# Value weights in column halves, a memory normalisation on ScalarE, and new ends for a two-layer decoder kernel

## The chip, the cores and the metric

The kernel runs on one core of a Trainium2 chip. The metric is the device time of one execution in microseconds. Before the change three runs gave a median of 1455.31 us, from 1453.81 to 1457.11 us.

## The reference, cut to what matters

The program is a decoder trunk of two layers on 256 tokens of width 1024, all in float32. Each layer is a half-step SwiGLU feed-forward part (FFN1), a mixer of four gated branches, a cross-attention into 256 memory tokens, and a second feed-forward part (FFN2). Each ends in `x = LayerNorm(alpha*x + f(x))`.

```python
mem_n = layer_norm(mem, mem_ln_g, mem_ln_b)            # once, for both layers
# mixer, branch a: local attention, 8 query heads on 2 key/value heads of 64, window 128, blocks of 128
p = exp(s - m); p = p / (sum(p) + exp(sink - m))
y_a = einsum('bngrqk,bnkgd->bnqgrd', p, vb).reshape(B, L, 512) @ swa_proj
# branch b: S5, a complex diagonal recurrence; branch d: differential attention
# branch c: gated depthwise convolution with 31 taps, LayerNorm over 512 channels, silu
y_c = conformer_conv(cu, ...) @ conv_proj
merged = g0 * y_a + g1 * y_b + g2 * y_c + g3 * y_d
x = layer_norm(alpha * x + merged @ w_out)
```

## The kernel before

**Weights.** Every large product is made of three TensorE passes (`mm3`): operands are split into a rounded part (hi) and the rest (lo), and hi*hi, hi*lo and lo*hi are added in PSUM. Weights come from HBM in raw halves of 128x1024, six at a time. For each half, called a split here and counted from 0 (236 per layer), ScalarE writes hi (a CAST) and VectorE writes lo (a TENSOR_TENSOR of the raw half and hi). `W.cap` bounds how many splits may be ahead of their use.

**Order.** All instructions are put in order when the program is built. A model of the engines' times (`Pace`, in `est`) is kept while instructions are issued; between matmuls `step()` looks whether the next task of a lane (local attention `swa`, differential attention `diff`, `s5`, `conv`, `taps`, the preparation lanes `prep`, `mem`, `bias`) is due by that model, and issues it. A task that says `yield` waits for its next turn. `ensure(name)` issues the rest of a lane at once. Taps of the convolution are put on VectorE (`fill`) when its modelled time falls behind TensorE's; what is left of them is flushed before the third gate's product, `gate(2)`. Each engine then runs its list strictly in that order, so a late instruction holds up all behind it.

**Local attention.** `swa_pv` multiplies the transposed probabilities (as the stationary operand, 128x128) with 64 columns of values (moving): 12 float32 matmuls per call, two calls per layer (query halves t = 0 and 1). ScalarE scales each 128x64 result by 1/sum into `osb`; `swa_end` transposes `osb` in eight blocks per layer and splits the result for `swa_proj`.

**Memory normalisation.** `mem_norm` runs once, in layer 0's FFN1, two row blocks: statistics and affine part on VectorE with gain and bias broadcast to two 512 KB tiles, then transposes, a split, and a store to DRAM that both cross-attentions read.

**Convolution.** After the flush, lane `conv` is issued within `gate(2)`, whose 96 matmuls are numbered from 0 here: `conv_norm` transposes the sum `c3` back to tokens (8 transposes), VectorE takes the statistics, GpSimd a power (`rstd`), ScalarE applies them (`Identity`, two of 512); `conv_act` transposes the result again (8 transposes); ScalarE makes a tanh and an affine copy (4 and 4 of 256, parameters `ph`), VectorE multiplies them, and both split them into `hT`, which `conv_proj`, the next product, reads.

**Ends.** The first product is `gate0` for token block c = 0: per chunk x-hi*w-hi and x-hi*w-lo, then all x-lo*w-hi at the end. The kernel's last work is the LayerNorm of token block 1 and four output stores from SyncE's queue.

Of the kernel before, what the change touches and what calls it, by code (L numbers as in the profile page):

```python
# [9 lines left out]
F32R = mybir.dt.float32r  # L10
# [3 lines left out]
ALU = mybir.AluOpType  # L14
# [168 lines left out]
def hybrid_decoder_kernel(ctx: ExitStack, tc: tile.TileContext, io, depth=DEPTH):  # L183
# [22 lines left out]
    def t2(dt=F32):  # L206
        return p2.tile([P, 512], dt, tag="s2", name="s2")
# [126 lines left out]

    def xs(xT, s, kc, c=None):

        if len(xT) == 3:
# [13 lines left out]
    class Norm:  # L351
# [22 lines left out]
        def finish(self, pump):  # L374
            self.scale()
            if pump:
                W.pump()
            self.apply(0)
            self.apply(1)
# [52 lines left out]
            run_task(name, q)  # L432


    def prod_tok(keys, xT, nk, before_c1=None, done=None, lo_last=False):

        hv = {}
        lo_last = lo_last or before_c1 is not None
        banks = [[None, None] for _ in keys]
        for c in range(2):  # L440
            for i, key in enumerate(keys):
                b = ps()
                for kc in range(nk):
                    if before_c1 and c == 0 and i == len(keys) - 1 and kc in (nk - 6, nk - 4):
                        before_c1((0,) if kc == nk - 6 else (1,))
                    if c == 0 and kc % 2 == 0:
                        hv[i, kc // 2] = W.take(key)
                    w = hv[i, kc // 2]
                    if lo_last and i == 0:
                        mm(b, xs(xT, 0, kc, c), w.h[:, kc % 2], kc == 0, False)  # L450
                        mm(b, xs(xT, 0, kc, c), w.l[:, kc % 2], False, False)
                        if kc == nk - 1:
                            for k in range(nk):
                                mm(b, xs(xT, 1, k, c), hv[i, k // 2].h[:, k % 2], False, k == nk - 1)
# [12 lines left out]
                if done:  # L467
                    done(i, c, b)
        return banks
# [18 lines left out]


    def ffn(xT, x, ln, before_c1, after_start=None, res=None, cap_end=CAP_FFN):  # L490
        gb, ub = prod_tok(("gate0", "up0"), xT, 8, before_c1)
        th = []
        for c in range(2):
            t = t2()
# [82 lines left out]
        for c in range(2):  # L577
            nm = block_norm(x[c], *w_ln)
            if c == 0:
                for h in range(2):  # L580
                    for (w2, gT), f in ((x_, f) for x_ in list(zip(ws, pend))[:-1] for f in range(2)):
                        out_mm(w2[f], gT, f, c, h)
                    if h == 0:
                        tick()
            for h in range(2):
                for i, (w2, gT) in enumerate(zip(ws, pend)):
                    if c == 0 and i < len(ws) - 1:
                        continue
# [9 lines left out]
            nm.finish(c == 1)  # L598
            if c == 0 and res is None:
                res = new_T()  # L600
        W.cap = CAP_FFN
# [4 lines left out]
    memD = dram.tile([P, 4096], F32, name="memT")  # L606

    def mem_norm():
        W.cap -= 2
        g, b = load_ln(io["mem_ln_g"], io["mem_ln_b"])  # L610
        mem = [t4(), t4()]
        for c in range(2):
            nc.sync.dma_start(out=mem[c], in_=m_in[0, c])
        yield 10.0
        for c in range(2):
            mt = mem[c]
            nm = Norm(mt, g, b, EPS)
            nm.half(0)
            nm.half(1)
            nm.scale()  # L620
            yield 1
            for h in range(2):
                nm.apply(h)
                yield 0
            for h in range(2):
                bk = transpose_blocks(mt[:, h * 512:(h + 1) * 512], 4)
                yield 0
                hi, lo = t2(F32R), t2(F32R)
                split_psum(bk, hi, lo)
# [4 lines left out]
        W.cap += 2  # L634

    memT = []

# [139 lines left out]
    def load_params():  # L777
# [4 lines left out]
        nc.sync.dma_start(out=rows[0:32], in_=io["s5_a_re"].rearrange("l (j a) p -> (l j) (a p)", a=2))  # L782
        nc.sync.dma_start(out=rows[32:64], in_=io["s5_a_im"].rearrange("l (j a) p -> (l j) (a p)", a=2))
        nc.sync.dma_start(out=rows[64:66], in_=io["diff_norm_g"])
        ls = sm(2)
        nc.sync.dma_start(out=ls[96:128], in_=io["s5_log_step"].rearrange("l (j a) -> (l j) a", a=2))
        r = 0
# [309 lines left out]
    def mixer(l, xT, x, before_c1, s5):  # L1097
# [324 lines left out]
        osb, dosb = [], []  # L1422

        def swa_scores(t, c):
            head = lambda r: (r // 2) * 4 + 2 * t + r % 2
# [9 lines left out]
        def swa_trans(t):  # L1435
            e0, e1, sums, d = att["a", t]
            r, o = inverse(sums, d), (t2(), t4())
            yield from transposed(o, e0, e1, 4)
            att["a", t] = (*o, r)

        def halves(o):
            if not o:
# [2 lines left out]
            return o  # L1445

        def swa_pv(t):
            halves(osb)
            o0, o1, r = att.pop(("a", t))
# [4 lines left out]
            for i in range(4):  # L1454
                g = i // 2
                for kb_ in range(2):
                    mm(b[:, 256 + i * 64:256 + (i + 1) * 64], o1[:, (2 * i + kb_) * P:(2 * i + kb_ + 1) * P], av[:, kb_, g * 64:(g + 1) * 64], kb_ == 0, kb_ == 1)
            yield 0
            for c in range(2):
                for k in range(4):  # L1460
                    S.activation(out=osb[c].rearrange("p (g u i d) -> p g u i d", g=2, u=2, i=2)[:, k // 2, t, k % 2],
                                 in_=b[:, c * 256 + k * 64:c * 256 + (k + 1) * 64], func=AF.Copy, scale=r[:, c * 4 + k:c * 4 + k + 1])

        def swa_end():
            aoT = L["aoT"] = (t4(F32R), t4(F32R))
            for c in range(2):
                b = transpose_blocks(osb[c], 4)
                yield 0
                o3 = [o.rearrange("p (k t) -> p k t", t=SEQ)[:, :, c * P:(c + 1) * P] for o in aoT]
                split_psum(b.rearrange("p (k t) -> p k t", t=P), o3[0], o3[1])  # L1470

        def attention_lane(name, scores, soft, mix, trans, pv, end):
            o = [(scores, 0, 1), (scores, 0, 0), (soft, 0), (scores, 1, 1), (scores, 1, 0), (mix, 0), (trans, 0), (soft, 1), (pv, 0), (mix, 1), (trans, 1), (pv, 1)]
# [3 lines left out]
            lane(name, [(("s", t) if f is scores else t, lambda f=f, t=t, k=k: f(t, *k)) for f, t, *k in o] + [(1, end)])  # L1477

        attention_lane("swa", swa_scores, swa_soft, None, swa_trans, swa_pv, swa_end)

        dkb = prod_feat("dk", xT, 8)
        dkT, dqT = t4(), t4()
# [86 lines left out]
        def project(key, oT, br, first=False):  # L1569
            gs = gates.pop(br)  # L1570
            if first:
                merged.extend([t4(), t4()])
            oT2 = [[oT[0]], [oT[1]], 1]
# [170 lines left out]
```

## Time and profile before

| | us |
|---|---|
| median of 3 runs (range) | 1455.31 (1453.81 to 1457.11) |
| the profiled execution | 1454.41 |
| its span in the trace | 1452.6 |
| TensorE busy | 1437.6 (99%) |
| VectorE busy | 1154.3 (79%) |
| ScalarE busy | 809.0 (56%) |
| GpSimd busy | 90.0 (6%) |
| HBM traffic | 188 GB/s over the span |

The span is the time from the first to the last instruction in the trace; 1.8 us of the execution lie around it. Busy time of TensorE counts pipelined matmuls and says that it is never idle for long, not that each matmul is as short as it can be. A row of a timeline gives start, length, engine, operation, output and inputs, and how many alike were joined; in brackets the idle time of that engine before the row and what ended it.

### The profile page before, as it was taken

What the parts mean: (1) busy time and instruction counts of PE and PEld (TensorE: products, weight loads), DVE (VectorE), ACT (ScalarE), POOL (GpSimd) and SP (SyncE); (2) the same over time, 40 slices, a digit from 0 to 9 for tenths busy, and PEclk for the clock granted to TensorE, in tenths of its full rate; (3) what the DMA queues carried; (4) which work ended last, traced back from release to release, by engine and by line L of the source; (5) the groups of instructions that cost most, each with busy time, mean ns of one, the idle gap of its engine ahead of it and who ended that gap; (6) DMA issues with size and microseconds to landing.
All of it is one profiled execution on the core that took longest, in us unless ns stands there. A gap on an engine that the chain in (4) does not pass through costs nothing.

```text
span 1452.6 us, 22933 instructions
## 1 busy us (share of the span) xinstructions
PE 1437.6 (99%) x8732; PEld 1236.0 (85%) x8732; DVE 1154.3 (79%) x1838; ACT 809.0 (56%) x1400; POOL 90.0 (6%) x113
## 2 busy tenths in 40 slices
PE   9999999999999999999999999999999999999997
PEld 6888889988887888888888888899888888888886
DVE  7789889898997878666788986839979887876665
ACT  6455543868956445444454555435988545444441
POOL 0300000101020000000000000010100300000000
PEclk9999999999999999999999999999999999999999
DMA  9766846544656756556665656555536577375650
GB/s 367 229 206 190 264 142 172 175 127 115 207 166 215 249 202 206 190 185 189 215 197 174 198 179 191 170 163 175 160 118 190 185 270 257 97 252 179 190 163 29
DMA packets 194197, 274.05 MB, mean 189 GB/s; under 512 B 38430, under 2 KB 118880, under 8 KB 194088
## 3 DMA queue, kind: packets, MB, share of 16 engines
q1 hardware_dynamic: 192488, 268.40, 58.1%
q0 software_dynamic: 1600, 4.20, 1.1%
q8 instruction: 68, 1.11, 0.3%
q14 instruction: 41, 0.34, 0.1%
HBM read 267.31 MB, written 5.24 MB: 188 GB/s over the span
## 4 chain that ended last, share of the span: by engine, by line
PE 92%; DVE 4%; ACT 2%; issue 1%; DMA 0%; SPq 0%; POOL 0%; POOLq 0%; DVEq 0%; ACTq 0%
PE b L177 92%; DVE s L177 4%; ACT s L177 2%; DMA raw<-in_ffn_w_in_dram 0%; DVE sm L177 0%; POOL sm L177 0%; SPq L69 0%; POOLq L1740 0%; DVE gpad L177 0%; DVEq L177 0%; SPq L285 0%; SPq L283 0%; ACTq L177 0%
## 5 line engine op out<-in xcount | busy, mean ns | idle before, releaser
L177 PE MATMUL b<-s,s 128*128 128x512 f32 (+3 forms) x8272 | 1405.6, 336 | 3.3 <-ACT s L177 1.8
L177 PEld LDWEIGHTS b<-s,s 128*128 128x128 f32 (+1 forms) x8272 | 1184.5, 183 | 192.2 <-issue 5.8
L177 DVE TENSOR_TENSOR s<-raw,s 128x1024 fp32r<-128x1024 f32 x472 | 570.3, 1232 | 114.5 <-ACT s L177 111.3
L177 ACT CAST s<-raw 128x1024 fp32r<-128x1024 f32 x472 | 483.1, 1055 | 62.8 <-DMA raw<-in_mix_w_in_dram 22.9
L177 ACT COPY s<-b 128x256 f32<-128x256 f32 (+2 forms) x216 | 93.9, 441 | 257.8 <-PE b L177 249.4
L177 DVE TENSOR_TENSOR s<-b,s 128x256 f32<-128x256 f32 (+3 forms) x264 | 115.2, 459 | 99.4 <-ACT s L177 91.5
L177 DVE TENSOR_TENSOR s<-s,s 128x512 f32<-128x512 f32 (+8 forms) x206 | 150.3, 735 | 35.4 <-ACT s L177 30.9
L177 ACT CAST s<-b 128x256 fp32r<-128x256 f32 (+1 forms) x100 | 36.9, 421 | 113.1 <-PE b L177 113.0
L177 POOL TENSOR_TENSOR sm<-sm,mhalf 128x1 f32<-128x1 f32 (+2 forms) x24 | 28.3, 1179 | 922.1 <-DVE sm L177 921.9
L177 ACT CAST s<-s 128x512 fp32r<-128x512 f32 x44 | 29.0, 669 | 93.2 <-DVE s L177 82.3
L177 ACT ACTIVATE s<-gpad,pc 128x256 f32<-128x256 f32 x152 | 66.2, 524 | 16.6 <-DVE gpad L177 16.6
L177 PE MATMUL b<-ident,s 128*128 128x128 f32 x449 | 64.9, 273 | 2.0 <-ACT s L177 1.9
L177 PEld LDWEIGHTS b<-ident,s 128*128 128x128 f32 x449 | 54.0, 141 | 12.6 <-ACT s L177 2.5
L177 DVE SCALAR_TENSOR_TENSOR s<-s,sm,s 128x512 f32<-128x512 f32 x72 | 52.5, 748 | 6.3 <-POOL sm L177 4.9
L177 ACT ACTIVATE s<-b,sm 128x64 f32<-128x64 f32 (+3 forms) x68 | 21.8, 396 | 47.9 <-DVE sm L177 43.8
L177 DVE SCALAR_TENSOR_TENSOR s<-gpad,pc,s 128x256 f32<-128x256 f32 x96 | 47.0, 541 | 0.6
L177 ACT ACTIVATE s<-b 128x512 f32<-128x512 f32 (+1 forms) x68 | 33.2, 533 | 13.1 <-PE b L177 13.1
L177 DVE SCALAR_TENSOR_TENSOR s<-s,s 128x512 f32<-128x512 f32 (+1 forms) x56 | 37.7, 685 | 0.4 <-ACT s L177 0.3
L177 ACT ACTIVATE s<-s 128x512 f32<-128x512 f32 (+1 forms) x52 | 32.2, 639 | 1.7 <-DVE s L177 1.7
L177 DVE SCALAR_TENSOR_TENSOR s<-s,b 128x512 f32<-128x512 f32 x40 | 26.2, 678 | 5.4 <-PE b L177 5.4
L177 ACT ACTIVATE s<-s,sm 128x128 f32<-128x128 f32 x64 | 28.4, 453 | 1.4 <-DVE sm L177 1.4
L177 DVE SCALAR_TENSOR_TENSOR s<-b,s 128x512 f32<-128x512 f32 x32 | 22.0, 687 | 8.2 <-PE b L177 8.1
(92 smaller groups left out, 305.5 us busy)
## 6 DMA issues: line engine op xcount, KB each, us to landing
raw<-in_ffn_w_in_dram SPq DMA_DIRECT2D x176, 512.0 KB, 3.9
raw<-in_mix_w_in_dram SPq DMA_DIRECT2D x116, 512.0 KB, 4.3
raw<-in_ffn_w_out_dram SPq DMA_DIRECT2D x88, 512.0 KB, 3.4
raw<-in_mix_w_out_dram SPq DMA_DIRECT2D x16, 512.0 KB, 5.2
raw<-in_cross_wkv_dram SPq DMA_DIRECT2D x16, 512.0 KB, 5.0
raw<-in_mix_w_in_dram SPq DMA_DIRECT2D x32, 128.0 KB, 4.3
raw<-in_swa_proj_dram SPq DMA_DIRECT2D x8, 512.0 KB, 5.2
raw<-in_diff_proj_dram SPq DMA_DIRECT2D x8, 512.0 KB, 5.1
```

Of the source, the lines that this page charges most:

```text
L177: return f(*a, **k)
```

## The change

1. `swa_trans` scales the probabilities by 1/sum before their transposes: four 128-wide ACTIVATEs on ScalarE and one 1024-wide multiply on VectorE per call. `swa_pv` makes the 64 value columns the stationary operand, placed at array columns 0 or 64 (`at=(0, 64*i)`), and the probabilities the moving one. The result is already transposed; it is split from PSUM, and `swa_end` with its transposes is gone.
2. `mem_norm` takes mean and variance with two ScalarE passes and normalises there; gain and bias come as columns of `pa` and are applied by ScalarE after the transposes. The two broadcast loads are gone, two loads of eight rows into `rows` are added, and `W.cap` is lowered by 1 instead of 2 meanwhile.
3. `gate0`, c = 0: first x-hi*w-hi and x-lo*w-hi for all chunks, then all x-hi*w-lo.
4. The last LayerNorm issues both subtract-and-scale steps before both steps with the power's result; the last output quarter is stored from ScalarE's queue.

```diff
@@ def swa_trans(t):
+            for i in range(4):
+                S.activation(out=e0[:, i * P:(i + 1) * P], in_=e0[:, i * P:(i + 1) * P], func=AF.Copy, scale=r[:, i:i + 1])
+            tt(V, e1.rearrange("p (i k) -> p i k", i=4), e1.rearrange("p (i k) -> p i k", i=4), r[:, 4:8].unsqueeze(2).to_broadcast([P, 4, 256]), ALU.mult)
+            yield 0
             yield from transposed(o, e0, e1, 4)
@@ def swa_pv(t):
-            for i in range(4):
-                g = i // 2
-                mm(b[:, i * 64:(i + 1) * 64], o0[:, i * P:(i + 1) * P], av[:, 0, g * 64:(g + 1) * 64])
...
+            for g in range(2):
+                for i in range(2):
+                    r = 2 * g + i
+                    mm(b[64 * i:64 * i + 64, g * 256:g * 256 + P], av[:, 0, g * 64:(g + 1) * 64], o0[:, r * P:(r + 1) * P], g == 0, True, skip=True, at=(0, 64 * i))
                 for kb_ in range(2):
-                    mm(b[:, 256 + i * 64:256 + (i + 1) * 64], o1[:, (2 * i + kb_) * P:(2 * i + kb_ + 1) * P], av[:, kb_, g * 64:(g + 1) * 64], kb_ == 0, kb_ == 1)
-            yield 0
-            for c in range(2):
-                for k in range(4):
-                    S.activation(out=osb[c].rearrange("p (g u i d) -> p g u i d", g=2, u=2, i=2)[:, k // 2, t, k % 2],
-                                 in_=b[:, c * 256 + k * 64:c * 256 + (k + 1) * 64], func=AF.Copy, scale=r[:, c * 4 + k:c * 4 + k + 1])
-        def swa_end():
...
+                    for i in range(2):
+                        r = 2 * g + i
+                        mm(b[64 * i:64 * i + 64, g * 256 + P:(g + 1) * 256], av[:, kb_, g * 64:(g + 1) * 64], o1[:, (2 * r + kb_) * P:(2 * r + kb_ + 1) * P],
+                           False, kb_ == 1, skip=True, at=(0, 64 * i))
+            yield 0
+            o = t4(F32R)
+            L.setdefault("aoT", []).append(o)
+            split_psum(b.rearrange("p (g n) -> p g n", g=2), *(o.rearrange("p (g s n) -> p g s n", g=2, s=2)[:, :, s] for s in range(2)))
@@ def mem_norm():
-        W.cap -= 2
-        g, b = load_ln(io["mem_ln_g"], io["mem_ln_b"])
+        W.cap -= 1
...
+            S.activation(out=junk, in_=mt, func=AF.Copy, scale=-1.0 / D, accum_out=m[:, 0:1])
+            S.activation(out=junk, in_=mt, func=AF.Square, bias=m[:, 0:1], accum_out=m[:, 1:2])
+            ts(V, r, m[:, 1:2], 1.0 / D, EPS, ALU.mult, ALU.add)
+            tt(G, r, r, mhalf[:, 0:1], ALU.pow)
+            tt(V, m[:, 1:2], m[:, 0:1], r, ALU.mult)
+            S.activation(out=mt, in_=mt, func=AF.Identity, scale=r, bias=m[:, 1:2])
...
+                for k in range(4):
+                    S.activation(out=y[:, f], in_=bk[:, f], func=AF.Identity, scale=pa[:, 66 + 4 * h + k:67 + 4 * h + k], bias=pa[:, 74 + 4 * h + k:75 + 4 * h + k])
@@ def prod_tok(keys, xT, nk, before_c1=None, done=None, lo_last=False, hi_first=False):
+                        first = hi_first and c == 0
+                        if first:
+                            mm(b, xs(xT, 1, kc, c), w.h[:, kc % 2], False, False)
+                        else:
+                            mm(b, xs(xT, 0, kc, c), w.l[:, kc % 2], False, False)
@@ class Norm: def finish(self, pump, last=False)
+            if last:
+                for h in range(2):
+                    stt(self.z[:, s], self.z[:, s], self.mv[:, 0:1], self.g[:, s], ALU.subtract, ALU.mult)
+                for h in range(2):
+                    stt(self.z[:, s], self.z[:, s], self.r, self.b[:, s], ALU.mult, ALU.add)
@@ end of the kernel
-            nc.sync.dma_start(out=o[0, c, :, h * 512:(h + 1) * 512], in_=x[c][:, h * 512:(h + 1) * 512])
+            (nc.scalar if c and h else nc.sync).dma_start(out=o[0, c, :, h * 512:(h + 1) * 512], in_=x[c][:, h * 512:(h + 1) * 512])
```

Since the order is worked out by the model, a change of one lane moves others. Three places follow; a name such as s_3504 is a tile of the program and b a PSUM bank.

On TensorE, in layer 0's mixer, the first `swa_pv` before (s_3101 holds the values, s_3504 and s_3505 the transposed probabilities):

```order
L177 MATMUL b<-s_3466,s_2030 128x512
L177 MATMUL b<-s_3101,s_3504 128x64 x4
L177 MATMUL b<-s_3101,s_3505 128x64 x8
L177 MATMUL b<-s_3517,s_2027 128x512
L177 MATMUL b<-s_3518,s_2027 128x512
```

and after the change (s_3166 holds the values, s_3710 and s_3711 the probabilities):

```order
L177 MATMUL b<-s_3760,s_2069 128x512
L177 MATMUL b<-s_3710,s_3166 64x128 x2
L177 MATMUL b<-s_3711,s_3166 64x128 x4
L177 MATMUL b<-s_3710,s_3166 64x128 x2
L177 MATMUL b<-s_3711,s_3166 64x128 x4
L177 MATMUL b<-s_3760,s_2069 128x512
```

Twelve matmuls stand in both; their outputs are now 64 partitions by 128 columns, the two columns halves of the array in turn.

On VectorE, at the end of layer 0's FFN1, between splits 72 and 73 (the rows with raw) before:

```order
L177 TENSOR_TENSOR s_2113<-raw,s_2112 128x1024
L177 TENSOR_TENSOR s_711<-pw 128x32 x2
L177 TENSOR_TENSOR pw<-s_711 128x32
L177 SCALAR_TENSOR_TENSOR pw<-pw 128x32
L177 TENSOR_TENSOR s_2127<-raw,s_2126 128x1024
```

and after:

```order
L177 TENSOR_TENSOR s_2153<-raw,s_2152 128x1024
L177 TENSOR_TENSOR s_637<-s_1830,s5k 128x256
L177 TENSOR_TENSOR s_638<-s_1831,s5k 128x256
L177 TENSOR_TENSOR s_1830<-s_637,s_638 128x16x16
L177 TENSOR_TENSOR s_637<-s_1831,s5k 128x256
L177 TENSOR_TENSOR s_638<-s_1830,s5k 128x256
L177 TENSOR_TENSOR s_1831<-s_637,s_638 128x16x16
L177 TENSOR_TENSOR s_2169<-raw,s_2168 128x1024
```

The S5 preparation is further along, and six products of 256 columns stand where four of 32 stood.

On TensorE, within layer 0's `gate(2)`, the end of `conv_act`'s transposes (from s_4882 and s_4884) before, the first of the 57 matmuls of the gate that follow them:

```order
L177 MATMUL b<-ident,s_4882 128x128
L177 MATMUL b<-ident,s_4884 128x128
L177 MATMUL b<-s_4765,s_2029 128x512
L177 MATMUL b<-s_4766,s_2029 128x512
L177 MATMUL b<-s_4765,s_2029 128x512
L177 MATMUL b<-s_4795,s_2030 128x512
L177 MATMUL b<-s_4796,s_2030 128x512
```

and after (from s_4952 and s_4954), up to the first matmul of `conv_proj`, which reads `hT` (s_4968):

```order
L177 MATMUL b<-ident,s_4954 128x128
L177 MATMUL b<-s_4857,s_2069 128x512
L177 MATMUL b<-s_4858,s_2069 128x512
L177 MATMUL b<-s_4857,s_2069 128x512
L177 MATMUL b<-s_4869,s_2070 128x512
L177 MATMUL b<-s_4870,s_2070 128x512
L177 MATMUL b<-s_4869,s_2070 128x512 x2
L177 MATMUL b<-s_4870,s_2070 128x512
L177 MATMUL b<-s_4869,s_2070 128x512
L177 MATMUL b<-s_4881,s_4968 128x512
```

The transposes of `conv_norm` stood behind matmul 18 of `gate(2)` and stand behind matmul 57; those of `conv_act` stood behind matmul 39 and stand behind matmul 87, nine matmuls ahead of `conv_proj`. In layer 1 the same two stood behind 21 and 42 and stand behind 30 and 54.

## Rows read from the trace of the kernel before

**Rows 1.** The page: busy time by engine, and shares of the chain that ended last.

```profile
PE 1437.6 (99%) x8732; PEld 1236.0 (85%) x8732; DVE 1154.3 (79%) x1838; ACT 809.0 (56%) x1400; POOL 90.0 (6%) x113
...
PE 92%; DVE 4%; ACT 2%; issue 1%; DMA 0%; SPq 0%; POOL 0%; POOLq 0%; DVEq 0%; ACTq 0%
```

**Rows 2.** TensorE's waits: us in total, times, longest us.

```profile
PE b L177 <- ACT s L177: 3.7, 3, 1.8
PE b L177 <- DVE s L177: 1.4, 2, 0.8
```

**Rows 3.** Timeline of TensorE at 267 us: S5 products of layer 0.

```profile
266.98 7.20 PE L177 MATMUL b<-s,s 64*64 64x64 f32 x98 [1.82 <-ACT s L177]
```

**Rows 4.** Windows: length, busy us (count) of PE, PEld, DVE, ACT, POOL, PEclk, DMA.

```profile
266.00:268.00 2.00, 1.02 (x34) 0.96 (x35) 1.24 (x2) 2.00 (x4) 0.00 (x0) 0.90 0.10 32
268.00:270.00 2.00, 2.00 (x37) 1.78 (x37) 2.00 (x4) 2.00 (x6) 0.00 (x0) 0.50 0.81 217
270.00:272.00 2.00, 2.00 (x24) 1.88 (x20) 2.00 (x4) 2.00 (x3) 0.00 (x0) 0.75 0.76 195
...
440.00:442.00 2.00, 2.00 (x13) 1.79 (x13) 1.23 (x2) 2.00 (x3) 0.00 (x0) 1.00 0.67 176
```

**Rows 5.** TensorE's groups by shape: rows*columns of the array, output, busy us, mean ns.

```profile
L177 PE MATMUL b<-ident,s 128*128 128x128 f32 x445 | 64.8, 273 | 2.0 <-ACT s L177 1.9 <-DMA s<-in_x_dram 0.2
L177 PE MATMUL b<-s,s 64*64 64x64 f32 x896 | 19.9, 225 | 1.8 <-ACT s L177 1.8
...
L177 PE MATMUL b<-s,s 128*128 128x64 f32 x96 | 11.2, 274 | 0.0
L177 PE MATMUL b<-s,s 64*128 64x256 f32 x64 | 9.1, 402 | 0.0
```

**Rows 6.** Timeline of ScalarE ahead of the S5 products.

```profile
265.79 1.14 ACT L177 COPY s<-s 128x768 f32<-128x768 f32 x2
```

**Rows 7.** Timeline of VectorE after split 72.

```profile
207.53 0.29 DVE L177 TENSOR_TENSOR s<-pw 128x32 f32<-128x32 f32 x2
...
208.07 1.22 DVE L177 TENSOR_TENSOR s<-raw,s 128x1024 fp32r<-128x1024 f32 x1
```

**Rows 8.** VectorE's group of S5 products by shape: busy us, mean ns.

```profile
L177 DVE TENSOR_TENSOR s<-s,s5k 128x256 f32<-128x256 f32 x64 | 24.3, 420 | 0.7
```

**Rows 9.** Timeline of TensorE in `gate(2)`, layer 0.

```profile
439.19 0.33 PE L177 MATMUL b<-ident,s 128*128 128x128 f32 x1 [1.51 <-ACT s L177]
439.86 0.98 PE L177 MATMUL b<-ident,s 128*128 128x128 f32 x7 [0.34 <-ACT s L177]
```

**Rows 10.** Timeline of ScalarE there: `conv_norm`, gate, `ph` and `hT`.

```profile
438.36 1.45 ACT L177 ACTIVATE s<-b,sm 128x512 f32<-128x512 f32 x2 [11.62 <-DVE sm L177]
...
444.32 1.12 ACT L177 ACTIVATE s<-b 128x512 f32<-128x512 f32 x2
445.29 1.97 ACT L177 ACTIVATE s<-b,ph 128x256 f32<-128x256 f32 x4
447.09 0.69 ACT L177 CAST s<-s 128x512 fp32r<-128x512 f32 x1
```

**Rows 11.** Timeline of VectorE: convolution taps in layer 0, and in layer 1.

```profile
417.69 3.06 DVE L177 SCALAR_TENSOR_TENSOR s<-gpad,pc,s 128x256 f32<-128x256 f32 x3
...
1097.33 2.46 DVE L177 SCALAR_TENSOR_TENSOR s<-gpad,pc,s 128x256 f32<-128x256 f32 x6
```

**Rows 12.** Timeline of TensorE in `gate(2)`, layer 1.

```profile
1149.41 5.04 PE L177 MATMUL b<-s,s 128*128 128x512 f32 x21
1154.29 1.03 PE L177 MATMUL b<-ident,s 128*128 128x128 f32 x8
```

**Rows 13.** Timeline of ScalarE there.

```profile
1152.40 1.45 ACT L177 ACTIVATE s<-b,sm 128x512 f32<-128x512 f32 x2 [9.78 <-DVE sm L177]
```

**Rows 14.** Timeline of ScalarE at the start.

```profile
12.53 1.05 ACT L177 CAST s<-raw 128x1024 fp32r<-128x1024 f32 x1 [1.52 <-DMA raw<-in_ffn_w_in_dram]
```

**Rows 15.** Timeline of VectorE at the end.

```profile
1447.12 2.20 DVE L177 SCALAR_TENSOR_TENSOR s<-s,sm,s 128x512 f32<-128x512 f32 x3 [0.44 <-POOL sm L177]
```

More of the change, by code (lines that the diff above doesn't have):

```diff
@@ L335, in xs @@
     def xs(xT, s, kc, c=None):
-        if len(xT) == 3:
+        if len(xT) == 2:
+            t = xT[kc % 2][:, (kc // 2) * 512 + s * SEQ:(kc // 2) * 512 + (s + 1) * SEQ]
+        elif len(xT) == 3:
             t = xT[s][0][:, kc * SEQ:(kc + 1) * SEQ]
@@ L372, in apply, with finish @@
             stt(self.z[:, s], self.z[:, s], self.r, self.b[:, s], ALU.mult, ALU.add)
-        def finish(self, pump):
+        def finish(self, pump, last=False):
             self.scale()
+            if last:
+                for h in range(2):
+                    s = slice(h * 512, (h + 1) * 512)
+                    stt(self.z[:, s], self.z[:, s], self.mv[:, 0:1], self.g[:, s], ALU.subtract, ALU.mult)
+                for h in range(2):
+                    s = slice(h * 512, (h + 1) * 512)
+                    stt(self.z[:, s], self.z[:, s], self.r, self.b[:, s], ALU.mult, ALU.add)
+                return
             if pump:
@@ L432, in ensure, with prod_tok @@
             run_task(name, q)
[L435 removed]
+    def prod_tok(keys, xT, nk, before_c1=None, done=None, lo_last=False, hi_first=False):
         hv = {}
@@ L449, in prod_tok @@
                     if lo_last and i == 0:
+                        first = hi_first and c == 0
                         mm(b, xs(xT, 0, kc, c), w.h[:, kc % 2], kc == 0, False)
-                        mm(b, xs(xT, 0, kc, c), w.l[:, kc % 2], False, False)
+                        if first:
+                            mm(b, xs(xT, 1, kc, c), w.h[:, kc % 2], False, False)
+                        else:
+                            mm(b, xs(xT, 0, kc, c), w.l[:, kc % 2], False, False)
                         if kc == nk - 1:
                             for k in range(nk):
-                                mm(b, xs(xT, 1, k, c), hv[i, k // 2].h[:, k % 2], False, k == nk - 1)
+                                mm(b, xs(xT, 0 if first else 1, k, c), hv[i, k // 2].l[:, k % 2] if first else hv[i, k // 2].h[:, k % 2], False, k == nk - 1)
                     else:
@@ L597, in ffn @@
                 W.free(6)
-            nm.finish(c == 1)
+            nm.finish(c == 1, c == 1 and res is False)
             if c == 0 and res is None:
@@ L614, in mem_norm @@
         yield 10.0
+        while "pa" not in prm:
+            yield 1
+        pa = prm["pa"]
+        junk = t4()
         for c in range(2):
[L616 to L623, printed above, removed]
-                yield 0
+            mt, m, r = mem[c], sm(2), sm(1)
+            S.activation(out=junk, in_=mt, func=AF.Copy, scale=-1.0 / D, accum_out=m[:, 0:1])
[5 more added lines that the diff above has]
+            tt(V, m[:, 1:2], m[:, 0:1], r, ALU.mult)
+            yield 0
+            S.activation(out=mt, in_=mt, func=AF.Identity, scale=r, bias=m[:, 1:2])
+            yield 0
             for h in range(2):
@@ L627, in mem_norm @@
                 yield 0
-                hi, lo = t2(F32R), t2(F32R)
-                split_psum(bk, hi, lo)
+                y, hi, lo = t2(), t2(F32R), t2(F32R)
+                for k in range(4):
+                    f = slice(k * P, (k + 1) * P)
+                    S.activation(out=y[:, f], in_=bk[:, f], func=AF.Identity, scale=pa[:, 66 + 4 * h + k:67 + 4 * h + k], bias=pa[:, 74 + 4 * h + k:75 + 4 * h + k])
+                yield 0
+                split_psum(y, hi, lo)
                 for s, t in enumerate((hi, lo)):
@@ L633, in mem_norm @@
                 yield 1
-        W.cap += 2
+        W.cap += 1
     memT = []
@@ L784, in load_params @@
         nc.sync.dma_start(out=rows[64:66], in_=io["diff_norm_g"])
+        nc.sync.dma_start(out=rows[66:74], in_=io["mem_ln_g"].rearrange("(k p) -> k p", p=P))
+        nc.sync.dma_start(out=rows[74:82], in_=io["mem_ln_b"].rearrange("(k p) -> k p", p=P))
         ls = sm(2)
@@ L1421, in mixer @@
         biasA, biasD = prm["biasA"], prm["biasD"]
-        osb, dosb = [], []
+        dosb = []
         def swa_scores(t, c):
@@ L1447, in swa_pv @@
         def swa_pv(t):
-            halves(osb)
-            o0, o1, r = att.pop(("a", t))
+            o0, o1 = att.pop(("a", t))
             b = ps()
-            for i in range(4):
-                g = i // 2
-                mm(b[:, i * 64:(i + 1) * 64], o0[:, i * P:(i + 1) * P], av[:, 0, g * 64:(g + 1) * 64])
-            for i in range(4):
-                g = i // 2
+            for g in range(2):
+                for i in range(2):
+                    r = 2 * g + i
+                    mm(b[64 * i:64 * i + 64, g * 256:g * 256 + P], av[:, 0, g * 64:(g + 1) * 64], o0[:, r * P:(r + 1) * P], g == 0, True, skip=True, at=(0, 64 * i))
@@ L1476, in attention_lane @@
                 ready[name, ("s", t)] = est["act"] + 0.3
-            lane(name, [(("s", t) if f is scores else t, lambda f=f, t=t, k=k: f(t, *k)) for f, t, *k in o] + [(1, end)])
-        attention_lane("swa", swa_scores, swa_soft, None, swa_trans, swa_pv, swa_end)
+            lane(name, [(("s", t) if f is scores else t, lambda f=f, t=t, k=k: f(t, *k)) for f, t, *k in o] + [(1, end)] * bool(end))
+        attention_lane("swa", swa_scores, swa_soft, None, swa_trans, swa_pv, None)
         dkb = prod_feat("dk", xT, 8)
@@ L1572, in project @@
                 merged.extend([t4(), t4()])
-            oT2 = [[oT[0]], [oT[1]], 1]
+            oT2 = oT if isinstance(oT, list) else [[oT[0]], [oT[1]], 1]
             for h in range(2):
```

13 lines of the change are left out of this document (4 added, 9 removed).

## Prediction

> **What bounds the kernel now.** I read the page first: TensorE is busy for 99% of the span and has 92% of the chain that ended last, VectorE 4% and ScalarE 2% [rows 1]. So a saving counts where it shortens TensorE's own list or removes a wait of it, and other work costs only where it makes TensorE wait. The table of TensorE's waits comes next: behind ScalarE it waited three times, 3.7 us in all and at most 1.8 us, and behind VectorE twice, 1.4 us in all, both at the start [rows 2]. The timeline places the three: 1.82 us at 267 us, ahead of S5's products in layer 0 [rows 3], and 1.51 and 0.34 us at 439 us, ahead of the transposes of `conv_act` in layer 0 [rows 9]. The windows show what the first brought with it: the granted clock, elsewhere full, fell to 0.5 (1.2 of 2.4 GHz) after that wait; the three windows at 0.90, 0.50 and 0.75 lost (0.10 + 0.50 + 0.25) x 2 = 1.7 us of matmul time. After the waits at 439 us it stayed at 1.00 [rows 4].
>
> **A, local attention.** Before, 96 records of products with 64 moving columns took 11.2 us, so 2.8 us for each of four calls [rows 5]. The change keeps 24 records per call, but each fills half of the array's columns. No row shows column halves. Row halves run beside each other: 64 records of 64x256 took 9.1 us, 0.142 us each, and 64x64 quadrants 19.9 / 896 = 0.022 us each [rows 5]. A record of row halves moves 256 columns and its pair takes 0.285 us; with 128 columns that is 0.142 us for a pair, entering and leaving the mode included. Twelve pairs then take 1.7 us and each call saves 1.1, together 4.4 us. The other end: one after the other, 24 x 0.142 = 3.4 us, each call loses 0.6 us. I take pairs, because the quadrants, which halve columns too, do run together.
>
> The Trainium skill, TensorEngine Tiling (Array Packing), Key Properties, says that tiles work in parallel but that changing the tiling mode drains TensorE. The rows on row halves and quadrants agree with the first part; the second is in them already. With pairs at half of before and no drain a call would take 1.4 us, and the whole would come out 1.2 us lower.
>
> Sixteen transposes go: at 64.8 / 445 = 0.146 us each 2.3 us [rows 5], of which I take 1.8, since the last of a group overlaps what follows. A is -4.4 - 1.8 = -6.2 us (bounds -6.7 and +0.6). What it adds lies beside TensorE: eight scalings on ScalarE per layer for sixteen narrower ones, and two 1024-wide multiplies on VectorE per layer, each 1.14 us at the pace of a split's lo (the 1.22 us row less its overlap [rows 7]). These come back under D.
>
> **B, memory normalisation.** VectorE loses the statistics and affine passes of both memory blocks in layer 0's FFN1, so the S5 preparation behind it comes earlier, as the order of split 72 shows. The S5 products that waited 1.82 us stand 116 matmul rows earlier in TensorE's list, and their last copies on ScalarE [rows 6] no longer stand behind convolution taps. I count this wait and the clock that it cost as gone: -1.8 - 1.7 = -3.5 us (other end 0: the same products wait at their new place). But six products of 256 columns now precede split 73: 6 x 24.3 / 64 = 2.3 us [rows 8], in place of 208.07 - 207.53 = 0.54 us [rows 7]. VectorE is held back there by the end of FFN1, not by earlier work, so its lead is worth nothing at this point. TensorE reads that lo soon after it ends; of 1.7 us I count 1.5 as a wait (bounds 0 and 1.7). B is -2.0 us.
>
> **C, the convolution in layer 0.** Less other work on VectorE does not end the flush sooner: twelve taps and three adds are left after split 138, where none was. So `conv_norm` and `conv_act` sit 39 and 48 matmuls later. The old waits of 1.51 + 0.34 us go [rows 9]. Late next is `hT`: before, 57 matmuls at (1154.29 - 1149.41) / 21 = 0.23 us [rows 12], 13 us, lay between the second transposes and `conv_proj`; now nine, 2.1 us. Lower bound of the new wait: after the last gate matmul ScalarE still has a tanh (half of 1.12), four `ph` steps (1.97) and the first hi (0.69) in its list [rows 10], 3.2 us, and a lo and the second half's hi and lo hold `conv_proj` by about 1.0 us more (the lo of 512 columns, half of a 1.22 us row, twice): 4.2 us. Upper bound: before, 447.78 - 439.81 = 8.0 us passed from the end of the normalised rows to the first hi [rows 10]; eight transposes (1.0) [rows 9] and nine matmuls cover 3.1, so 4.9 + 1.0 = 5.9 us. I take 5.3, nearer to the upper end, as ScalarE's list is the same. Whether the clock falls too: a wait of 1.82 us was followed by half clock, waits of 1.51 and 0.34 were not [rows 4]. I count half of 1.7 us. C is -1.85 + 5.3 + 0.85 = +4.3 us.
>
> The Trainium skill, TensorE: Matmul & The Clock Gate, Part 1, has the throttled clock as the default and activity as what releases it. [...]
>
> **D, the convolution in layer 1.** Two multiplies and one more split stand before the statistics: 3.4 us more on VectorE. `conv_act` comes twelve matmuls (2.8 us) later but TensorE is 3.1 us ahead by A. Before, the normalised rows ended at 1153.85 [rows 13] and the transposes began unheld at 1154.29 [rows 12], 0.44 us of slack. So the wait lies between 0 and 3.4 + 0.3 - 0.4 = 3.3 us, by how much of VectorE's earlier idle time takes up the work; I take 1.5. After it 42 matmuls (9.7 us) cover the 8 us chain.
>
> **E and F, the ends.** At the start TensorE waited 1.4 us for lo parts [rows 2]; they are needed later now, but raw halves still arrive one by one (1.52 us of waiting for one [rows 14]) and the fifth gates the next product: -0.2 us (bounds 0 and -1.4). At the end VectorE's 0.44 us of waiting for the power [rows 15] is filled: -0.4 us. Storing from ScalarE's queue has no row; the four stores wait for VectorE anyway, so 0 (bounds -0.3 and +0.5).
>
> **Sum.** -6.2 - 2.0 + 4.3 + 1.5 - 0.2 - 0.4 = -3.0 us. The profiled execution took 1454.41 us, so 1451.4 us; this execution lies 0.9 us under the median of 1455.31.
>
> **Rivals.**
> 1. *VectorE has slack at the new places.* For it: VectorE's list has less work up to split 130, and its busy share is 79% [rows 1]. Against it: at split 73 the end of FFN1 sets its start. No waits at 73 and in layer 1, no fall of the clock, 4.2 us at `conv_proj`: -6.2 - 3.5 + 2.35 - 0.6 = -8.0, 1446.5 us.
> 2. *Slower: column halves run one after the other.* The place is the four `swa_pv`; it costs 0.6 us per call instead of saving 1.1, so A is +0.6 and the sum +3.8, 1458.2 us. It decides from 0.20 us for a pair on: the rest of the sum is +3.2 without A, the transposes give 1.8, and a call of 12 x 0.204 = 2.45 us saves only 0.35, four times 1.4. For it: no row has column halves. Against it: the quadrants.
> 3. *The convolution is late in both layers.* The tap on VectorE took 1.02 us in one place and 0.41 in another [rows 11]; if some of the flush runs at the former, split 139's lo comes about 1.2 us late, `hT` is at its upper bound, the clock falls and layer 1 pays in full: C is 5.9 + 1.2 + 1.7 - 1.85 = +6.95, D +3.3, the sum +1.6, 1456.0 us.
> 4. *The wait at 267 us only moves.* B is +1.5 and the sum +0.5, 1454.9 us. For it: its copies on ScalarE remain; against it: the order.
>
> **How the numbers follow.** The forecast has 43%, the rivals 22, 10, 14 and 11%. Times within 0.2% (2.9 us) cannot be told from no change. The forecast lies just at that border: about 0.6 of its share is faster, with rival 1 and a little from the others 50%. Slower are most of rival 2, the tail of rival 3 and a little of the others: 13%. The rest, 37%, is no change. By itself the forecast's range is 1449 to 1454; reaching to rival 1 and to rival 3 and most of rival 2 gives 1446.5 to 1457.5.
>
> **What would show it.** Right: records of 64x128 in column halves at some 0.07 us each; no wait near 267 us and full clock there; a wait of 1 to 2 us near split 73's use (about 209 us); one of 4 to 6 us where layer 0's `conv_proj` begins, behind ScalarE; at most 3 us at layer 1's second convolution transposes. Wrong: no wait ahead of `conv_proj`, or a PV call longer than 2.8 us.

## The result: 0.5% slower

The changed kernel took 1462.57 us in the median of 4 runs (1461.48 to 1462.66), beside 1454.93 us for the kernel before. The ratio is 1.0051, with a 95% interval of 1.0039 to 1.0063. The prediction was 1451.4 us, with 1446.5 to 1457.5 us as its range: the time lies above it, and the change is a loss where a gain was forecast.

The page of the changed kernel (busy time by engine, shares of the chain that ended last; to be read beside [rows 1]):

```profile
span 1460.9 us, 22901 instructions
...
PE 1435.4 (98%) x8716; PEld 1229.0 (84%) x8716; DVE 1155.3 (79%) x1830; ACT 819.5 (56%) x1410; POOL 91.7 (6%) x113
...
PE 90%; DVE 6%; ACT 1%; issue 1%; DMA 1%; SPq 0%; DVEq 0%; ACTq 0%
```

TensorE works 2.2 us less and the span is 8.3 us longer, so the loss is waiting. Its waits (us in total, times, longest us), where [rows 2] had 3.7 and 1.4 us:

```profile
PE b L177 <- DVE s L177: 10.1, 5, 6.7
PE b L177 <- ACT s L177: 4.8, 3, 3.8
PE b L1698 <- DVE s L1694: 1.2, 1, 1.2
PE b L177 <- DMA s<-in_x_dram: 1.1, 1, 1.1
```

The timeline of TensorE, the rows with a wait of over half a microsecond after the start (answering to [rows 3, 9, 12]):

```profile
211.87 28.88 PE L177 MATMUL b<-s,s 128*128 128x512 f32 x191 [1.66 <-DVE s L177]
...
443.95 1.22 PE L177 MATMUL b<-s,s 128*128 128x512 f32 x2 [6.70 <-DVE s L177]
...
461.01 10.30 PE L177 MATMUL b<-s,s 128*128 128x512 f32 x36 [3.76 <-ACT s L177]
...
1158.89 1.16 PE L177 MATMUL b<-ident,s 128*128 128x128 f32 x6 [1.08 <-DVE s L177]
```

The wait of 267 us is gone. Two new ones stand in layer 0's third gate and before `conv_proj`, and the windows behind them (columns as in [rows 4]) show half clock after each, where the one stretch at 268 us was:

```profile
444.00:446.00 2.00, 2.00 (x7) 1.70 (x8) 2.00 (x2) 0.00 (x0) 0.00 (x0) 0.50 0.26 80
446.00:448.00 2.00, 2.00 (x9) 1.71 (x8) 1.97 (x4) 0.00 (x0) 0.00 (x0) 0.51 0.83 275
...
462.00:464.00 2.00, 2.00 (x5) 1.55 (x6) 0.97 (x2) 1.63 (x3) 0.00 (x0) 0.50 1.04 411
464.00:466.00 2.00, 2.00 (x8) 1.58 (x7) 0.14 (x1) 0.88 (x1) 0.00 (x0) 0.74 0.38 145
```

While TensorE was busy these stretches lost 3.6 us (2.0 in the first two windows, 1.6 around the second wait), against 1.6 us before. The account: TensorE's waits 17.2 us instead of 6.5 (+10.7), half clock +2.0, its own work 1435.4 - 3.6 instead of 1437.6 - 1.6 us (-4.2): +8.5 us, for the 8.3 us of the spans.

What stood in TensorE's way is on VectorE's timeline in layer 0, around the flush:

```profile
429.79 1.27 DVE L177 SCALAR_TENSOR_TENSOR s<-s,b 128x512 f32<-128x512 f32 x2
430.99 1.99 DVE L177 TENSOR_TENSOR s<-s,s 128x1024 f32<-128x1024 f32 x1
433.01 5.75 DVE L177 SCALAR_TENSOR_TENSOR s<-gpad,pc,s 128x256 f32<-128x256 f32 x12
438.87 3.88 DVE L177 TENSOR_TENSOR s<-s,s 128x1024 f32<-128x1024 f32 x3
442.67 4.63 DVE L177 TENSOR_TENSOR s<-raw,s 128x1024 fp32r<-128x1024 f32 x4
```

The last row is the low parts of splits 139 to 142. The first of them ends at 443.8 us and TensorE goes on at 443.95. It had read split 138 until 437.25 us; split 139's low part stood behind the flush, an add at 430.99 us, twelve taps and three adds. TensorE had begun the gate at 424.6 us (437.25 less 55 matmuls at 0.23 us), 6.4 us before the first of these.

VectorE had not been busy all the time before that. The window from 300 to 430 us, before and after (columns as in [rows 4]):

```profile
300.00:430.00 130.00, 130.00 (x994) 109.50 (x993) 122.60 (x212) 100.47 (x233) 14.90 (x20) 1.00 0.50 149
```

```profile
300.00:430.00 130.00, 129.87 (x887) 107.87 (x886) 115.78 (x208) 108.80 (x247) 19.00 (x18) 1.00 0.54 163
```

VectorE was busy for 94% of it before, and for 89% after: it idled 6.8 us more and had its taps left over at the end. What it waited for in this window, before

```profile
DVE s L177 <- ACT s L177: 6.5, 7, 1.9
DVE s L177 <- PE b L177: 0.5, 1, 0.5
```

and after:

```profile
DVE s L177 <- ACT s L177: 10.3, 11, 2.1
DVE s L177 <- PE b L177: 3.1, 3, 2.0
```

### The profile page after: what moved, and what is told of

It is laid out like the page before. It is cut to its first block, busy times and chain, and to the rows that moved or that the text cites. A ratio compares the mean times of both kernels' runs of the same rounds, so it can differ in the third digit from the quotient of the medians.

```text
span 1460.9 us, 22901 instructions
## 1 busy us (share of the span) xinstructions
PE 1435.4 (98%) x8716; PEld 1229.0 (84%) x8716; DVE 1155.3 (79%) x1830; ACT 819.5 (56%) x1410; POOL 91.7 (6%) x113
## 4 chain that ended last, share of the span: by engine, by line
PE 90%; DVE 6%; ACT 1%; issue 1%; DMA 1%; SPq 0%; DVEq 0%; ACTq 0%
PE b L177 90%; DVE s L177 6%; ACT s L177 1%; DMA raw<-in_ffn_w_in_dram 1%; DMA raw<-in_cross_wo_dram 0%; SPq L69 0%; DVE sm L177 0%; DVEq L1762 0%; DVEq L177 0%; SPq L288 0%; SPq L285 0%; SPq L283 0%; ACTq L177 0%
## 5 line engine op out<-in xcount | busy, mean ns | idle before, releaser
L177 PE MATMUL b<-s,s 128*128 128x512 f32 (+5 forms) x8272 | 1404.7, 336 | 14.0 <-DVE s L177 8.9
L177 PEld LDWEIGHTS b<-s,s 128*128 128x128 f32 (+3 forms) x8272 | 1178.3, 183 | 206.7 <-DVE s L177 11.5
L177 DVE TENSOR_TENSOR s<-s,s 128x512 f32<-128x512 f32 (+8 forms) x210 | 157.1, 755 | 36.2 <-ACT s L177 30.2
L177 PE MATMUL b<-ident,s 128*128 128x128 f32 (+1 forms) x433 | 64.0, 275 | 2.4 <-DVE s L177 1.2
L177 PEld LDWEIGHTS b<-ident,s 128*128 128x128 f32 (+1 forms) x433 | 52.9, 142 | 14.0 <-DVE s L177 2.0
L177 DVE SCALAR_TENSOR_TENSOR s<-s,sm,s 128x512 f32<-128x512 f32 x64 | 46.4, 748 | 5.5 <-POOL sm L177 4.4
L177 ACT ACTIVATE s<-s,sm 128x128 f32<-128x128 f32 (+1 forms) x84 | 38.2, 474 | 10.7 <-DVE sm L177 10.7
L177 ACT ACTIVATE s<-b,sm 128x128 f32<-128x128 f32 (+2 forms) x36 | 14.8, 460 | 41.3 <-DVE sm L177 41.3
L177 ACT ACTIVATE s<-s 128x512 f32<-128x512 f32 (+2 forms) x54 | 34.2, 650 | 0.8 <-DVE s L177 0.8
L177 POOL TENSOR_TENSOR s<-s,s 128x512 f32<-128x512 f32 x16 | 25.0, 1582 | 65.9 <-DVE s L177 41.9
```

Of the source, the lines that this page charges most:

```text
L177: return f(*a, **k)
```

## The experiments

**Which part.** Theory 1: the flush of twelve taps and adds ahead of split 139 is the loss. The first runs take the parts singly, and the whole change with another order.

Run 1, the whole change with one constant altered. A tap is issued while VectorE's modelled time is less than `FILL` us ahead of TensorE's, so a larger `FILL` issues taps sooner:

```diff
-FILL = 2.0
+FILL = 6.0
```

> The whole change with one constant altered: FILL is 6.0 instead of 2.0, so that the convolution's taps are issued on VectorE earlier and none is left to flush before layer 0's third gate. Same instructions, another order. Theory 1 (the flush ahead of the low parts of the gate's second half is what costs): the waits of 6.70 and 3.76 us at 444 and 461 us and the two stretches of half clock behind them (about 3.5 us) go or stay under 2 us together; 1449 to 1452 us. Rival (VectorE simply has too much to do in the mixer, beside GpSimd's adds, wherever the taps stand): the waits move to other low parts or to the statistics; at least 7 us of TensorE waits remain in layer 0's mixer and the time stays at 1458 us or more.

It took 1470.88 us (ratio 1.0113, 1.0099 to 1.0127). Nothing was left to flush and the two waits were gone, but waits of 4.65 us at 409 us and 3.85 us at 1136 us behind ScalarE, and smaller ones, came instead. Taps and adds put in earlier would stand ahead of the small steps and low parts for which ScalarE and TensorE wait; that is the likely reason, and no row shown here proves it. Theory 1 as a matter of the flush alone fell.

Run 2, only the attention of the change (the diff of `swa_trans` and `swa_pv`, without the rest):

> Only the local attention of the change (value columns as weights, scaled probabilities), all else as before. Three taps are left to the flush in either layer. Theory 1: no wait over 2 us in layer 0's third gate; TensorE's own list is 5 to 6 us shorter, the wait at 267 us stays; 1449 to 1452 us. Rival (the two multiplies on VectorE per layer make the convolution late): waits of over 5 us at the convolution, 1456 us or more.

It took 1461.60 us (1.0049, 1.0036 to 1.0061): the rival's number, though not the wait of over 5 us at the convolution that it named. Its longest wait stands at the step between the S5 branch and its gate:

```profile
402.61 3.50 PE L177 MATMUL b<-s,s 128*128 128x256 f32 x17 [3.59 <-DVE s L177]
```

Three taps were left to flush, and three waits of 1.36, 0.54 and 1.07 us stood at the convolution.

Run 3, only the memory normalisation (the diff of `mem_norm` and its two loads):

> Only the memory normalisation of the change. Five taps and two adds are left to the flush in layer 0 (twelve and four in the whole change, none before). Theory 1: the wait at 267 us goes (3.5 us with its clock), a wait of about 1.6 us comes at 212 us, and a wait of 1 to 4 us before the low part of the fourth half of the gate's second product in layer 0 with a smaller one at conv_proj; 1455 to 1459 us. Rival: no slower than before minus 2 us, that is 1453 us or less.

1457.20 us (1.0019, 1.0010 to 1.0028), the time that theory 1 had. The waits came otherwise: none before the fourth half's low part, and the larger one at `conv_proj`. They are 1.66 us at 212 us, and

```profile
439.42 1.09 PE L177 MATMUL b<-ident,s 128*128 128x128 f32 x8 [0.69 <-DVE s L177]
...
454.58 5.77 PE L177 MATMUL b<-s,s 128*128 128x512 f32 x20 [2.52 <-ACT s L177]
```

The second is `conv_proj` waiting for `hT`, as the prediction's part C described it, at a flush of five taps and two adds.

Run 4, only the order of the first product (the diff of `prod_tok`):

> Only the new order of the first product (hi of both operands first, the low parts of the weights last). The prediction's term was -0.2 us. The trace after shows TensorE 0.5 to 0.7 us later at 20 us, with 1.1 us of waiting for x from DMA against 0.2 us. If that is the run's own: 1454 to 1455 us, same. If the new order costs it: 1455.5 us or more.

1453.30 us (0.9997, 0.9988 to 1.0006): no difference clear of the noise. The later start in the trace after goes with that execution's wait of 1.1 us for x, which this trace does not have.

**What it is.** Theory 2: VectorE, not TensorE, sets the pace of layer 0's mixer up to the convolution, so that what TensorE saves turns into waiting. Runs 5 and 6 take 12 of the 31 taps out of the kernel before and of the changed one (the result lacks these taps):

```diff
-        for k in range(1, 31 - ACT_TAPS):
+        for k in range(7, 31 - ACT_TAPS):
-            for k in range(31 - ACT_TAPS, 31):
+            for k in range(37 - ACT_TAPS, 31):
```

> The kernel before, with 12 of the convolution's 31 taps left out in both layers (6 on VectorE, 6 on ScalarE with their adds on VectorE): VectorE has about 17 us less work in each mixer. Theory 2 (VectorE, not TensorE, sets the pace of layer 0's mixer up to the convolution, so what TensorE saves there becomes waiting): TensorE was nearly gap-free already, so only the 1.85 us at the convolution go; 1451 to 1454 us. Rival (the order that the model makes is what costs): the same.

> The whole change with the same 12 taps left out. Theory 2: with VectorE relieved, TensorE's savings arrive: no wait over 1 us in either mixer but for the 1.66 us at 212 us, and 4 to 9 us less than the kernel before with fewer taps; 1443 to 1449 us. Rival (the loss comes from the moved order, whatever VectorE's load): at most 2 us less than the kernel before with fewer taps, or more.

Before with fewer taps took 1453.85 us (0.9997, 0.9988 to 1.0006), the change with fewer taps 1445.08 us (0.9932, 0.9919 to 0.9944). The same change that costs 7.6 us gains 8.8 us once VectorE and ScalarE have less to do. Run 13 leaves ScalarE's taps whole and takes out only 8 of VectorE's adds of them per layer (these taps do not reach the result):

```diff
-                fill.insert(0, lambda: tt(V, c3, c3, busy.pop(), ALU.add))
+                if k < 39 - ACT_TAPS:
+                    busy.pop()
+                else:
+                    fill.insert(0, lambda: tt(V, c3, c3, busy.pop(), ALU.add))
```

> The whole change with the adds of 8 of ScalarE's 18 taps left out in both layers (ScalarE still makes them): VectorE 8 x 1.14 = 9.1 us less per layer, ScalarE's work whole. Theory 2, VectorE alone decides: no wait over 1 us at layer 0's third gate and conv_proj, 1444 to 1449 us. Rival (ScalarE's list counts as much): waits behind ScalarE of 3 us or more remain in the mixers, 1453 us or more.

1444.76 us (0.9930, 0.9916 to 0.9943), with these waits of TensorE in the whole span, of which 1.67 us are the one at 211 us:

```profile
PE b L177 <- DVE s L177: 2.3, 2, 1.7
PE b L1701 <- DVE s L1697: 1.2, 1, 1.2
PE b L177 <- ACT s L177: 0.7, 1, 0.7
```

So ScalarE's work need not shrink: leaving out adds on VectorE alone, an estimated 9.1 us per layer, is worth 17.8 us to the changed kernel. To the kernel before, 12 taps less were worth some 1 us (run 5), which is within the noise.

This does not part load from order. With less to place, the model also put the convolution sooner: `conv_norm`'s transposes, behind 57 matmuls of layer 0's `gate(2)` in the changed kernel, stand behind 12 in run 13, with nothing flushed,

```profile
426.31 1.03 PE L177 MATMUL b<-ident,s 128*128 128x128 f32 x8
```

and behind 15 in run 6. For load speaks that no other order of the whole change (runs 1, 8, 10 and 12) came under the kernel before.

Run 9 does the opposite: the kernel before with the change's two multiplies per layer on VectorE, their result unused:

```diff
             att["a", t] = (*o, r)
+            tt(V, e1.rearrange("p (i k) -> p i k", i=4), e1.rearrange("p (i k) -> p i k", i=4), r[:, 4:8].unsqueeze(2).to_broadcast([P, 4, 256]), ALU.mult)
```

> The kernel before with one useless 1024-wide multiply per call of swa_trans on VectorE (two per layer, after the probabilities' transposes), as many as the change adds; TensorE's list is untouched. Theory 2 (VectorE sets the pace of layer 0's mixer): each 1.14 us of VectorE's work there is paid, partly with a half-clock stretch behind a longer wait: 1457 to 1462 us. Rival (VectorE has room): 1454 to 1456 us.

1456.06 us (1.0006, 0.9997 to 1.0015): a miss for theory 2 in its strict form. Two multiplies per layer alone cost about 1 us, and 2.2 us at the end of the interval; VectorE had a little room. That it takes both, more work on VectorE and a TensorE that arrives sooner, is inferred: no run has the second without a change in VectorE's or ScalarE's work.

Run 7, the added multiply on ScalarE instead:

```diff
-            tt(V, e1..., r[:, 4:8].unsqueeze(2).to_broadcast([P, 4, 256]), ALU.mult)
+            for i in range(4):
+                S.activation(out=e1[:, i * 256:(i + 1) * 256], in_=e1[:, i * 256:(i + 1) * 256], func=AF.Copy, scale=r[:, 4 + i:5 + i])
```

> The whole change, with the 1024-wide multiply of each call on ScalarE as four 256-wide passes: VectorE 2.3 us less per layer. The flush before layer 0's third gate shrinks to four adds. Theory 2: the 6.70 us wait falls to 0 to 3 us and the total to 1454 to 1459 us. Rival (the convolution comes late in the order in any case and ScalarE's added work delays the weights' casts): waits of 8 us or more remain, 1461 us or more.

1460.14 us (1.0033, 1.0021 to 1.0046), between the two ranges and so a miss for both. The 6.70 us became 1.50 us, as theory 2 had it, but 3.69 us before `conv_proj` stayed and 1.95 us behind ScalarE came in layer 1.

Run 8, the flush spread over the gate's matmuls:

```diff
-        while fill or lanes["taps"]:
...
+        def flush():
+            while fill or lanes["taps"]:
+                for _ in range(2):
+                    if fill:
+                        fill.pop(0)()
...
+                yield 0
...
+        lane("conv", [(0, flush), (0, conv_norm), (0, conv_act)])
```

> The whole change, with the flush of layer 0's and layer 1's last taps spread over the third gate's matmuls, two taps at a time, in place of all before it. Theory 1 (the low part of the gate's fourth half stands behind the flush): the 6.70 us wait falls under 1.5 us, but the convolution is finished later, and the wait before conv_proj grows from 3.8 to 6 to 12 us; 1458 to 1465 us. Theory 2 says the same sum: VectorE's work until the convolution's end is unchanged.

1462.15 us (1.0051, 1.0038 to 1.0063), within the range. The waits did not go as expected (under 1.5 us, and 6 to 12 us before `conv_proj`) but were cut up: 3.91 us at 441 us, 1.97 us at 456 us, 3.50 us before `conv_proj`. Here the place of the flush moved TensorE's waits and left the time the same.

**The other wait, and whole kernels.** Run 10, the whole change with the preparation lanes held while the first mixer product is issued:

```diff
+        quiet[0] = l == 0
         dvb, g3b = prod_tok(("dv", "gl"), xT, 8, before_c1)
+        quiet[0] = False
```

> The whole change, with the preparation lanes held until layer 0's first mixer product is issued, so that no S5 products stand between splits 72 and 75. If the 1.66 us wait at 212 us is those products: it goes, and with it 1.7 us at most. By theory 2 the gain is eaten at the convolution, since VectorE's work is the same: 1460 to 1464 us, the wait before the gate's second half or before conv_proj the longer for it. Rival (TensorE's waits simply add): 1460.5 us or less with the later waits unchanged.

1457.97 us (1.0020, 1.0011 to 1.0029): under theory 2's range, and within the rival's, though the later waits did not stay as the rival had them. The 1.66 us wait went, which shows its cause. The flush became ten taps without adds, and the 6.70 us fell to five waits of 0.58 to 1.20 us between 403 and 440 us; `conv_proj` still waited 2.36 us.

Runs 11, 12 and 15 add to run 10's holding of the lanes a `FILL` at which nothing is left to flush: without the attention (2.5), with all (3.0), and with all and the multiplies on ScalarE (2.5).

> The change without its local attention, the preparation lanes held as above, and FILL 2.5: no taps are left to flush. VectorE has about 8 us less work than before and the wait at 267 us is gone. Theory 2: the convolution of layer 0 is no later than before; 1449 to 1453 us. Rival (any change of order costs as much as it gains): 1455 us or more.

> The whole change, the preparation lanes held as above, and FILL 3.0: no taps are left to flush in either layer. Theory 1 (the late flush is the cost): 1447 to 1452 us. Theory 2 (VectorE's total work in the mixers is): the waits move to low parts of weights earlier in layer 0's mixer, as with FILL 6.0; 1456 to 1466 us.

> The whole change, the preparation lanes held until layer 0's first mixer product is issued, the added multiplies on ScalarE, FILL 2.5 (nothing left to flush). VectorE's work in the mixer is that of before. Theory 2: close to the relieved kernel in layer 0, 1449 to 1454 us; rival (ScalarE becomes late): waits behind ScalarE of 4 us or more, 1456 us or more.

They took 1455.30 us (1.0005, 0.9997 to 1.0014), 1461.28 us (1.0044, 1.0031 to 1.0056) and 1459.80 us (1.0034, 1.0022 to 1.0047). Runs 11 and 15 are misses for theory 2, and their times are the rivals': in run 11 VectorE had less work than before and nothing was gained, and in run 15 it had as much as before, ScalarE had more, and the loss stayed. The last two waited 6.70 and 4.63 us behind ScalarE at 406 and 409 us. Run 12's ScalarE there

```profile
402.55 2.03 ACT L177 CAST s<-s 128x512 fp32r<-128x512 f32 x2 [2.08 <-DVE s L177]
405.86 1.14 ACT L177 ACTIVATE s<-b,sm 128x128 f32<-128x128 f32 x4 [1.27 <-DVE sm L177]
```

waits for VectorE in its turn. Run 16, run 12 with the merged branches' adds on VectorE, took 1460.39 us with a wait of 6.69 us there, again the rival's time.

Run 14, the kernel before with those adds moved from GpSimd:

```diff
-                        tt(G, merged[c][:, s], merged[c][:, s], gs[c][:, s], ALU.add)
+                        tt(V, merged[c][:, s], merged[c][:, s], gs[c][:, s], ALU.add)
```

> The kernel before with the merged branches' adds on VectorE in place of GpSimd. In the trace after, two adds on GpSimd (3.5 us) stretch VectorE's work beside them by about 2.0 us (two lo parts 3.44 for 2.28 us, an add of 1024 1.95 for 1.14); on VectorE they take about 1.2 us. If that is so VectorE is about 3 us ahead by the convolution of each layer and the 1.85 us wait goes: 1452 to 1454.5 us. Rival (the stretch is hidden in waits anyway, and four more instructions per branch are not): 1455 to 1458 us.

1454.01 us (0.9993, 0.9984 to 1.0002): within what was expected, but not clear of no change; one of the two waits at 439 us fell from 1.51 to 0.72 us.

Two complete kernels came out a little faster. Run 17 has the new attention in layer 1 only and both ends; run 18 is run 14 with both ends.

> The new attention in layer 1 only, and the two ends; memory normalisation and layer 0's attention as before. Theory 2: layer 0 as before; in layer 1 TensorE's 2.5 to 3 us are saved and 1 to 2 us lost again at the convolution's second transposes; 1452 to 1454 us. Rival (the attention's reordering costs in any layer): 1456 us or more.

> The kernel before with the merged branches' adds on VectorE and the two new ends. If run 14's 1.0 us, run 4's start and the 0.4 us at the end add up: 1452.5 to 1454 us, faster than before by 1 to 2.5 us.

1452.99 us (0.9990, 0.9981 to 0.9999) and 1452.07 us (0.9986, 0.9978 to 0.9995): both under the kernel before, by 0.1%, with intervals that end just under 1. In layer 1 alone the new attention brings no loss.

## Why the prediction was wrong

**A was right.** The 96 records of the values' products take 6.1 us instead of the 11.2 of [rows 5]:

```profile
L177 PE MATMUL b<-s,s 128*64 128x128 f32 x96 | 6.1, 277 | 0.0
```

That is 0.064 us for a record, and 5.1 us saved for a predicted 4.4: column halves run side by side. This agrees with the Trainium skill, TensorEngine Tiling (Array Packing), Key Properties, which has tiles work in parallel. The transposes, 64.8 us before, take 2.0 us less in run 13, for a predicted 1.8:

```profile
L177 PE MATMUL b<-ident,s 128*128 128x128 f32 x429 | 62.8, 274 | 0.0
```

Rival 2 was wrong.

**B was right, its clock term by luck of the trace.** The wait at 267 us went, and the one at split 73 came with 1.66 us for a predicted 1.5. Run 10 shows its cause. The 1.7 us for the clock belong to the execution that was profiled: in five of the other traces that have this wait the clock stayed full behind it (last section).

**D, E and F were about right.** In layer 1 the transposes waited 0.16 + 1.08 us for a predicted 1.5. The start is within the noise (run 4). At the end the four steps of VectorE follow one another

```profile
1454.80 2.73 DVE L177 SCALAR_TENSOR_TENSOR s<-s,sm,s 128x512 f32<-128x512 f32 x4
```

in 2.7 us, where the first began 3.4 us before the end of the row in [rows 15].

**The step that failed is C.** It priced one new wait, 5.3 us before `conv_proj` and half a stretch of half clock, +4.3 us in all. That wait came, with 3.76 us, under its lower bound of 4.2: TensorE went on behind the first hi of `hT`, which ends at 460.95 us, and the 1.0 us for the lo and the second half was not paid.

```profile
460.28 0.67 ACT L177 CAST s<-s 128x512 fp32r<-128x512 f32 x1
```

What C put at nothing, without a reason, was a wait for split 139's low part, though it names the flush that stands ahead of it. Only rival 3 has it, as 1.2 us (and its sum comes to +1.45 us, not +1.6); it was 6.70 us. With two stretches of half clock (3.6 us) and the old 1.85 us gone, C is +12.2 us. The flush was known in size, but nothing in C says when VectorE gets to it. From the first add to the end of the low part it took 12.8 us (430.99 to 443.8), and TensorE needed that part 12.65 us after it had begun the gate: had both begun together, the part would have been just in time. But VectorE began 6.4 us later (430.99 against 424.6). Up to there it had idled 6.8 us more than before from 300 to 430 us, waiting more for ScalarE and TensorE. The signs that the prediction listed for being right came or nearly came, so they could not have told: none of them was about split 139.

The sum without C and D, -6.2 - 2.0 - 0.2 - 0.4 = -8.8 us, is what runs 5 and 6 differ by: 8.8 us. That the two are equal is partly luck: TensorE's busy time falls by 6.9 us (1437.6 to 1430.7), somewhat more than A's 6.2, while B's place gives only 0.2 us there, a wait of 1.84 us with the clock full in run 5 for one of 1.66 us. But the savings are real, and the kernel before has little room on VectorE to let them through. Its busy share of 79% [rows 1] hid 94% in that stretch. That was rival 1's ground, and it was read from the wrong row.

What stays open: whether VectorE's load or the order that the model makes of it is the loss, and which of VectorE's waits from 300 to 430 us are due to that order and which to the order that data needs. No run held the order fixed.

## What to carry to other kernels

A saving on the busiest engine counts only where the next engine has room, and the share of the span does not show that. Nor does the share of the stretch by itself: from 300 to 430 us VectorE was busy for 94% before, for 89% in the changed kernel and for 91% in run 13, and only the second had the long waits. What counts is when the engine gets to the work that others wait for. Where a planner leaves work over to be flushed, look at what stands behind the flush on its engine, and count from when that engine gets there in the trace, lag included. Before a change is judged, take load from the second engine in both versions: the pair shows whether the saving is lost or was never there, though where a planner makes the order, it moves the order too.

## Of the hardware

The length of a wait of TensorE did not tell whether half clock followed. Half clock followed waits of 6.70 and 3.76 us (changed kernel) and 3.59 us (run 2), but also of 2.36 and 1.10 us (run 10) and of 0.87 us (run 15, at 310 us); behind 2.52 us in run 3 the clock stayed full. Ahead of the S5 products at 267 us the same wait of 1.80 to 1.85 us was followed by half clock in the traces of the kernel before [rows 3, 4] and of runs 9 and 17, and not in those of runs 2, 4, 5, 14 and 18.

GpSimd's adds go with longer steps on VectorE: two low parts that take 2.35 us alone took 3.44 us at 426 us in the changed kernel, where the first ran beside

```profile
424.12 3.53 POOL L177 TENSOR_TENSOR s<-s,s 128x512 f32<-128x512 f32 x2 [2.96 <-DVE s L177]
```

and took 2.31 us. In run 14, with these adds on VectorE, the low parts there take 1.22 us each; the move was worth about 1 us, not clear of the noise.
